# Hybrid SSD and attention layer on one core: small copies and constants change engines, and three pieces of side work change places

## The chip, the core and the metric

The kernel runs on one core of a Trainium2 chip. Its time is device time in microseconds (us), the median of several executions. A profile of one execution gives the times below; they count from the first instruction (the span). TensorE is PE in the profile, VectorE DVE, ScalarE ACT, GpSimd POOL, SyncE (which issues the DMAs) SP.

## What is computed

One decoder layer in float32 on 16 learned meta tokens and 1024 tokens of width 1024. Cut to what matters here:

```python
xn = rms_norm(h, mix_pre_g)                       # (1040, 1024)
z, xbc, dt_raw, q, k, v = split(xn @ w_in)
xbc = silu(causal_dwconv(xbc, conv_w, conv_b))    # 4 taps; x, B (2 groups), C (2 groups)
dt = softplus(dt_raw + dt_bias);  Acs = cumsum(dt * A)      # "decays", by chunk
y_ssd = rms_norm((intra_chunk(C, B, exp(seg(Acs)), x*dt) + C @ state * exp(Acs) + x*D) * silu(z))
beta = sigmoid(q @ k.T / 8)                       # stick breaking, strictly causal, 16 heads
w[t, s] = beta[t, s] * prod(1 - beta[t, j] for s < j < t)
y_sb = rms_norm(w @ v)
h = h + rms_norm(concat(y_ssd, y_sb) @ w_out)
h = h + rms_norm((gelu(causal_dwconv3(xn2 @ w_g)) * (xn2 @ w_u)) @ w_down)
```

## The kernel before

Every large product is made of three matmuls on a high and a low part of both operands. ACT makes the high part of a weight tile (whi, L182), POOL the low part (wlo, L183). Pairs of tiles are multiplied by a scheme of seven products in place of eight (class Duo); each product takes 24 matmuls of 128x260 and ends in an add on VectorE (L321) or a copy on ACT (L318). The raw result of a block that is convolved is a tile craw_* of 1043 columns, whose first three columns are zero.

The instructions of each engine run in the order in which the program writes them. A DMA of SP also stands in its queue, behind the DMAs written before it. The stages, in us of the span:

- 0 to 62: tokens are normed and transposed; the first blocks B0 and C0 are projected. Their convolutions remain to be done.
- 62 to 360: thirteen duos: x00, z00, x02, z02, bc, x10, z10, x12, z12 and four of q and k. While duo i runs its seven products, the list `slots` holds side work, `slots[j]` being issued behind product j. A convolution in it is cut into taps (L495 the first, L498 the others), a silu with a store (L502, L504) and three transposes with copies (`turns`). dt_acts is the softplus and the decays: `dts[3]` ends in L667, `dts[4]` to `dts[6]` are the decays (pz, L674) and a transpose of the cumulative sum (tacs).
- 360 to 449: the V projection.
- 449 to 605: the scan, 18 units of a group and a chunk. Its start makes three pairs of constants sl and sg, into which DMAs write the cumulative sums. A unit's weights are a difference of cumulative sums by matmul (sg, L1051), relu and exp on ACT (em), a matmul of C and B (cb, L1075) and a product on VectorE (em, L1081); yt (L1117) is their use. In between stand steps of a generator `fill` (the remaining q and k projections, pj_q and pj_k, six matmuls a step, 128 steps in all; SCAN_FILL sets how many a unit takes). A finished accumulator goes into a tile st: ACT makes the high part (L922), VectorE the low part (L928) or, with `via_sbuf`, ACT a copy sw (L925) and POOL the low part. A store (qkd<-st, L913) frees st. The tiles st are a ring of two, zk and xd (loads from L1037) rings of three.
- 605 to 905: the attention, 64 blocks (a pair of heads, 128 queries). A block's scores z (L1275) go through a sigmoid on ACT (kp, L1276) and a running product on VectorE (kp, L1279). Three blocks later comes its turn: transposes on TensorE (tw, L1296) and a copy of 1 - tw into th, on ACT for the first half (L1301), on VectorE for the second (L1299). th is the weight of the product with v (av, L1314). Further fill steps and pieces of the output projection stand between.
- 905 to 1734: output projection, FFN and down projection, in which the change does nothing.

Of the kernel before, what the change touches and what calls it, by code (L numbers as in the profile page):

```python
# [9 lines left out]
F32 = mybir.dt.float32  # L10
F32R = mybir.dt.float32r
BF16 = mybir.dt.bfloat16
AF = mybir.ActivationFunctionType
# [4 lines left out]
P = 128  # L18
# [17 lines left out]
QH = [QC[0], QC[2], QC[3], QC[1]]  # L36
NA = (NT + 1) * 16
NQA = 4
SCAN_FILL = 44
OUT_FILL = 14  # L40
FILL_AT = (2, 1)
BLOCKS = (7, 0, 6, 1, 5, 2, 4, 3)
# [25 lines left out]
def tile_layer(ctx: ExitStack, tc: tile.TileContext, x, meta, rows, parts,  # L68
# [158 lines left out]
    def raw_tile(nm, zero=False):  # L227
        raw = sr.tile([P, L + 3], F32, tag="cr", name=f"craw_{nm}", bufs=4)
        if zero:
            nc.gpsimd.memset(raw[:, 0:3], 0.0)  # L230
        return raw

    def conv_chain(nm, w, halves_=4):
# [498 lines left out]
    def merged(*lists):  # L732
        return [sum(parts_, []) for parts_ in zip(*lists)]

    c0_taps, _ = conv_acts(10, chains[1][0], "C0", None, bcd[0][1])
    dts = dt_acts()
    slots = [b0_taps[:2] + dts[0], b0_taps[2:4], b0_taps[4:] + c0_taps[:2], c0_taps[2:4], c0_taps[4:] + b0_turns[:1],
             b0_turns[1:2], b0_turns[2:], dts[1]]
    for i, q in enumerate(duos):
        n = duos[i + 1] if i + 1 < len(duos) else None  # L740
        if i + 2 < len(duos):
            duos[i + 2].load()
        for j, m in enumerate((1, 5, 2, 6, 7, 3, 4) if i == 0 else (1, 6, 5, 7, 2, 3, 4)):
            q.product(m)
            if i == 0:
                if m == 1:
                    d0.split_4()
                elif m == 6:
                    split_t(t4l.bitcast(F32), xo["t4"], nc.vector)
            if n is not None:  # L750
                if m == 1:
                    n.split_22()
                elif m == 6:
                    n.sums()
                elif m == 7:
                    n.split_3()
                elif m == 2:
                    n.split_1()
                elif m == 3:
                    n.split_4()  # L760
            elif m in (7, 2):
                v_split(1, int(m == 2))
            for act in slots[j]:
                act()
        extra = slots[7:]
        slots = q.done(q)
        for k, acts_ in enumerate(extra):
            slots[k] = acts_ + slots[k]
        if i == 1:
            slots = merged(slots, [[], dts[2], [], dts[3], [], [], dts[4]]) + [dts[5], dts[6]]  # L770
        if i == n_early:
            t_stack.close()
            vl = v_stack.enter_context(tc.tile_pool(name="vl", bufs=1, side="left"))
            fetch_v(1, 0, vl)
        if i + 2 == len(duos):
            fetch_v(0, 0, None)
# [138 lines left out]
    def qk_fill():  # L915
        def chain(n, qs):
            which, p = qk_blocks[n]

            def ev(acc, c0, m):
                put_stores()  # L920
                st = st_pool.tile([P, 2, CQ], F32R, tag="st", name=f"st{which}{p}{c0}")
                nc.scalar.activation(st[:, 0, :m], acc[:, :m], AF.Copy)  # L922
                if via_sbuf[0]:
                    raw = st_pool.tile([P, CQ], F32, tag="sw", name=f"sw{which}{p}{c0}", bufs=1)
                    nc.scalar.activation(raw[:, :m], acc[:, :m], AF.Copy)  # L925
# [58 lines left out]
    with tc.tile_pool(name="ssd", bufs=1, side="right") as sp:  # L984
# [22 lines left out]
        for b in range(3):  # L1007
            sl = sp.tile([32, P], F32R, tag=f"sl{b}", name=f"sl{b}")
            sg = sp.tile([32, 8, P], F32R, tag=f"sg{b}", name=f"sg{b}")
            nc.scalar.activation(sl, ones[:32], AF.Copy)  # L1010
            pick = sp.tile([32, 8], F32, tag="pick", name=f"pick{b}")
            nc.vector.tensor_tensor(pick, ident[:32, 16:24], ident[:32, 24:32], op=ALU.add)
            nc.scalar.activation(sg, pick.unsqueeze(2).to_broadcast([32, 8, P]), AF.Copy, scale=-1.0)
            segs.append((sl, sg))

        def load_bc(g, c):
# [14 lines left out]
        def load_zx(g, c):  # L1031
            a, b = (M0, NM) if c == 0 else (NM + (c - 1) * P, NM + c * P)
            y0 = M0 if c == 0 else 0
            zx = []
            for t, d in (("zk", zd), ("xd", xdd)):
                zx.append(sp.tile([P, 4, P], F32, tag=t, name=f"{t}{g}_{c}", bufs=3))
                nc.sync.dma_start(out=zx[-1][:, :, y0:y0 + b - a], in_=d[g][:, :, a:b].rearrange("b p t -> p b t"))  # L1037
            zxs[g, c] = zx

# [111 lines left out]
            run(fill, n * SCAN_FILL // 27 - (n - 1) * SCAN_FILL // 27)  # L1151

        load_bc(*units[0])
        nc.sync.dma_start(out=dtk, in_=dtkd)
        load_x(*units[0])
        load_state(0, 2)
        load_bc(*units[1])
        load_x(*units[1])
        load_bc(*units[2])
# [7 lines left out]
        for n, (g, c) in enumerate(units):  # L1167
# [13 lines left out]
            yt, zk, xd, prev[g] = chunk_outputs(g, c, *cur)  # L1181
            if nxt:
                chunk_mask(*units[n + 1], *nxt)
            via_sbuf[0] = int(n > 16)
            scan_fill()
            if late_sq:
                late_sq.pop(0)()
# [6 lines left out]
            elif n > 14:  # L1194
                load_q(n - 15)
            cur = nxt
        late_sq.pop(0)()
        chunk_sum(NT)

    roll = ExitStack()  # L1200
# [87 lines left out]
    def block_turn(p, i, bt, ths):  # L1288
        nm = f"{p}_{i}"
        for u in range(i // 4 + 1):  # L1290
# [4 lines left out]
                    c0 = (4 * u + b) * P  # L1295
                    nc.tensor.transpose(tw[:, j, b, :], bt[:, j, c0:c0 + P], ident)  # L1296
            th = ap.tile([P, 2, 4, P], F32, tag="th", name=f"th{nm}_{u}", bufs=4)
            if u:
                nc.vector.tensor_scalar(th[:, :, :nb, :], tw[:, :, :nb, :], -1.0, 1.0, op0=ALU.mult, op1=ALU.add)  # L1299
            else:  # L1300
                copied[0] = nc.scalar.activation(th[:, :, :nb, :], tw[:, :, :nb, :], AF.Copy,  # L1301
# [158 lines left out]
    def out_steps(half, t, w, y, evac):  # L1460
        yh, yl = y
        for hf in range(2):
            acc = psum_mm(f"mo{half}_{t}_{hf}")
            cs = slice(512 * hf, 512 * hf + 512)
            for k, (wh, wl) in enumerate(w):
                if k and k % 2 == 0:
                    yield 0
                for j, (u, v) in enumerate(((yh, wh), (yl, wh), (yh, wl))):
# [1 line left out]
            evac(acc, cs)  # L1470
            yield 1

    stage_tile = [lambda name: st_pool.tile([P, 2, CQ], F32R, tag="st", name=name).bitcast(F32)
                  .rearrange("p a b -> p (a b)")[:, :512]]

    def ssd_half(w, ys):
# [50 lines left out]
            closed[0] = next(work, 1)  # L1527

    shares = [FILL_AT[i % 2] * (4 if i < 2 else 1) for i in range(8 * NT)]
    total = 2 * (64 - 8 - SCAN_FILL) + 9 + 2 * OUT_FILL  # L1530

    def share(n):
        return round(total * sum(shares[:n]) / sum(shares))
# [5 lines left out]
    for step in range(8 * NT):  # L1539
# [12 lines left out]
        due = mix[:1]  # L1552
        if len(turn) >= TURN_LAG:
            run(begin_turn())
        if step == 0:
            some(5)
        block = block_weights(p, i)
        next(block, None)
        if p > 0 and n == 4:
# [891 lines left out]
```

## Time and profile before

| | |
|---|---|
| three executions, us | 1736.82, 1739.46, 1734.83 (median 1736.82) |
| the profiled execution, us | 1736.27 (span 1734.6, 1.7 around it) |
| busy: PE, DVE, ACT, POOL, us | 1672.1, 1098.9, 741.5, 768.1 |
| TensorE's mean granted clock | 0.991 |

A row of the waits gives who waited and on which line, for whom, the us in total, how often, and the longest. A row of the timeline gives the start, the us of that row, the engine, the line and tiles, and in brackets the idle time just before with what ended it; a row may join several instructions (x2). A group (by line and shape) gives the count, the busy us and mean ns, and behind the bar the idle time before. A row of windows gives a stretch, its length, the busy us of PE (and of PEld, DVE, ACT and POOL, where all engines are asked for), the clock granted to TensorE, where 1.00 is full, and the DMA's share and rate. Line numbers are those of the kernel before; in the changed kernel they are higher by 1 from about L1010 and by 2 from about L1240.

### The profile page before, as it was taken

To read this page: it belongs to the slowest core of one execution; us is meant where nothing else is said; L and a number is where in the kernel's file an instruction comes from. 1 tells how busy PE (TensorE), PEld (TensorE's weight loads), DVE (VectorE), ACT (ScalarE), POOL (GpSimd) and SP (SyncE) were. 2 spreads that over 40 slices of the span, in tenths; PEclk is the share of its full clock that TensorE was granted. 3 is DMA by queue.
4 is the path that set the end of the run, shared out by engine and by line. 5 is a ranking of instruction groups with operands and counts; after the bars stand their busy time and mean duration, and the time that the engine had idled before them with its cause. 6 is when DMAs were issued, how large, how long until landed. Compare 5 with 4: busy or idle time off the path is not lost.

```text
span 1734.6 us, 29010 instructions
## 1 busy us (share of the span) xinstructions
PE 1672.1 (96%) x11508; PEld 1438.2 (83%) x11508; DVE 1098.9 (63%) x1279; ACT 741.5 (43%) x1110; POOL 768.1 (44%) x591
## 2 busy tenths in 40 slices
PE   6899999999999999899999999999999999999998
PEld 5899999978777777677777788999998888888887
DVE  7756544354166687977771367676666656658777
ACT  6444344332244355655553344533333333344544
POOL 3665766620267452324322212487776677400001
PEclk9999999999899999999999999999999999999999
DMA  5334334434478764443422654233332222296335
GB/s 197 132 135 126 112 122 147 154 120 158 135 227 244 213 201 145 147 125 102 131 75 95 236 181 153 67 116 104 95 113 97 92 92 91 95 330 206 104 104 188
DMA packets 164522, 247.40 MB, mean 143 GB/s; under 512 B 18489, under 2 KB 99489, under 8 KB 162706
## 3 DMA queue, kind: packets, MB, share of 16 engines
q1 hardware_dynamic: 164386, 245.54, 43.9%
q8 instruction: 91, 1.49, 0.4%
q14 instruction: 45, 0.37, 0.1%
HBM read 162.00 MB, written 83.47 MB: 142 GB/s over the span
## 4 chain that ended last, share of the span: by engine, by line
PE 75%; DVE 5%; issue 4%; ACT 3%; POOL 2%; DMA 2%; SPq 0%; DVEq 0%; POOLq 0%; ACTq 0%
PE fX L1855 10%; PE mo L1469 10%; PE dnA L2267 7%; PE fY L1855 7%; PE fA L1855 7%; PE dnB L2267 5%; PE av L1314 3%; PE z L1275 2%; DVE kp L1279 2%; PE pj_k L219 2%; PE tw L1296 2%; PE dXqk L309 2%; PE vB L812 2%; PE pj_q L219 2%; PE dYqk L309 1%
## 5 line engine op out<-in xcount | busy, mean ns | idle before, releaser
L1279 DVE TENSOR_TENSOR_SCAN kp<-kp,hold 128x344 f32<-128x344 f32 (+6 forms) x224 | 198.1, 944 | 42.5 <-ACT kp L1276 42.1
L183 POOL TENSOR_TENSOR wlo<-wr,whi 128x1024 fp32r<-128x1024 f32 x43 | 99.3, 2319 | 41.0 <-ACT whi L182 37.5
L2304 POOL TENSOR_TENSOR fms<-fms 128x1 f32<-128x1 f32 x8 | 2.3, 288 | 222.0 <-DMA ar<-fda 185.9
L182 ACT ACTIVATE whi<-wr 128x1024 fp32r<-128x1024 f32 x43 | 45.7, 1062 | 112.2 <-PE fX L1855 73.5
L1927 DVE SCALAR_TENSOR_TENSOR ga<-gr,pp,ga 128x1024 f32<-128x1024 f32 x44 | 69.3, 1575 | 34.3 <-ACT ga L1920 33.6
L1254 POOL TENSOR_SCALAR cb<-kp 128x32 f32<-128x32 f32 x64 | 37.8, 591 | 117.1 <-DVE kp L1279 110.1
L2189 ACT ACTIVATE dh<-ar 128x512 fp32r<-128x512 f32 x77 | 48.6, 631 | 94.8 <-PE dnB L2267 44.7
L1276 ACT ACTIVATE kp<-z 128x688 f32<-128x688 f32 (+6 forms) x112 | 78.8, 736 | 14.9 <-PE z L1275 13.9
L1296 PE MATMUL tw<-ident,kp 128*128 128x128 f32 x576 | 76.8, 278 | 7.0 <-DVE th L1299 2.9
L2190 DVE TENSOR_TENSOR dl<-ar,dh 128x512 fp32r<-128x512 f32 x77 | 53.2, 691 | 47.2 <-ACT dh L2189 47.2
L1314 PEld LDWEIGHTS av<-th,v 128*64 128x64 f32 x1152 | 62.3, 138 | 22.4 <-issue 11.5
L1275 PE MATMUL z<-k,q 64*128 64x348 f32 (+8 forms) x672 | 75.2, 345 | 4.0 <-DVE th L1299 2.5
L1314 PE MATMUL av<-th,v 128*64 128x128 f32 x1152 | 77.8, 280 | 0.5 <-ACT ysc L1317 0.5
L1296 PEld LDWEIGHTS tw<-ident,kp 128*128 128x128 f32 x576 | 62.1, 141 | 17.1 <-issue 6.9
L1301 ACT ACTIVATE th<-tw 128x1024 f32<-128x1024 f32 x64 | 55.3, 864 | 34.5 <-PE tw L1296 33.1
L1275 PEld LDWEIGHTS z<-k,q 64*128 64x128 f32 x672 | 52.1, 186 | 20.9 <-issue 9.5
L2267 PE MATMUL dnA<-dl,dh 128*128 128x512 f32 x176 | 68.5, 389 | 0.0
L2267 PE MATMUL dnA<-dh 128*128 128x512 f32 x176 | 68.5, 389 | 0.0
L2267 PE MATMUL dnA<-dh,dl 128*128 128x512 f32 x176 | 68.5, 389 | 0.0
L1988 POOL TENSOR_TENSOR al<-wr,ah 128x512 fp32r<-128x512 f32 x20 | 28.6, 1432 | 77.5 <-ACT ah L1987 77.4
L2267 PE MATMUL dnB<-dh 128*128 128x512 f32 x132 | 51.3, 389 | 0.0
L2267 PE MATMUL dnB<-dh,dl 128*128 128x512 f32 x132 | 51.3, 389 | 0.0
(999 smaller groups left out, 6076.3 us busy)
## 6 DMA issues: line engine op xcount, KB each, us to landing
wr<-in_w_up SPq DMA_DIRECT2D x44, 512.0 KB
fds<-ga SPq DMA_DIRECT2D x44, 256.0 KB
b<-in_w_down SPq DMA_DIRECT2D x44, 256.0 KB
ar<-fds SPq DMA_DIRECT2D x44, 256.0 KB
fda<-ga SPq DMA_DIRECT2D x33, 256.0 KB
ar<-fda SPq DMA_DIRECT2D x33, 256.0 KB
k<-qkd SPq DMA_DIRECT2D x8, 1040.0 KB
q<-qkd SPq DMA_DIRECT2D x64, 128.0 KB
```

The source lines that it names most:

```text
L183: nc.gpsimd.tensor_tensor(l, raw, h.bitcast(F32), op=ALU.subtract)
L219: mm(acc[:, :CQ - s], a[:, k, :], b[:, k % 4, c + s:c + CQ], start=(k == 0 and j == 0), stop=(k == KB - 1 and j == 2))
L1275: mm(z[:, j, :w], u[h, :], r[h, a:a + w], start=s_ == 0, stop=s_ == 2)
L1276: nc.scalar.activation(kp[:, :, a:a + w], z[:, :, :w], AF.Sigmoid, scale=-QSCALE)
L1279: nc.vector.tensor_tensor_scan(part, part, hold[:, L - n + a:L - n + a + w][:, ::-1], 1.0 if ci == 0 else kp[:, j, a + w:a + w + 1], op0=A ...
L1296: nc.tensor.transpose(tw[:, j, b, :], bt[:, j, c0:c0 + P], ident)
L1301: copied[0] = nc.scalar.activation(th[:, :, :nb, :], tw[:, :, :nb, :], AF.Copy, scale=-1.0, bias=1.0).ins
L1314: mm(av[halves[j], :], v[:, kb, halves[j]], th[:, j, b, :], start=kb == 0, stop=kb == i)
L1469: recent[0] = mm(acc, u[:, k, :], v[:, cs], start=(k == 0 and j == 0), stop=(k == 7 and j == 2))
L1855: mm(acc[:, c, :nn], u[:, k, :], v[:, k, c0:c0 + nn], start=first and k == 0 and j == 0, stop=k == 3 and j == 2, skip_group_check=not first)
L1927: nc.vector.scalar_tensor_tensor(v, self.g[jj][:, :, i:i + 256], fconv_w[:, j, i:i + 1], v, op0=ALU.mult, op1=ALU.add)
L2267: mm(banks[BANK[n], t], u[:, 0, c], v[:, 1, :], start=(n in (1, 2, 5) and p == 0 and i == 0), stop=(p == NPR - 1 and i == 2), skip_group_c ...
```

## The change

1. The three zero columns of craw_* are written by ACT, no longer by POOL (12 instructions).
2. In the first duo the four taps of C0 stand two places later, and its silu with them.
3. The decays dts[4] to dts[6] stand one place later.
4. At the scan's start sl is written by POOL and sg by VectorE, both by ACT before; the loads of the states (B and C) stand ahead of the loads of dtk and x. st is a ring of three, xd a ring of two.
5. Of the fill steps, 82 stand inside the scan where 88 stood, and six at its end, ahead of chunk_sum; some(5) at the attention's first step is gone, and its steps come later in the same step, behind the first scores. Behind unit 16, VectorE makes the low parts where ACT's copy sw and POOL did.
6. The turn's second half is copied by VectorE only while left is 0. left is the number of finished halves of the last q and k block.

```diff
-SCAN_FILL = 44
+SCAN_FILL = 41
...
         if zero:
-            nc.gpsimd.memset(raw[:, 0:3], 0.0)
+            nc.scalar.activation(raw[:, 0:3], ones[:, 0:3], AF.Copy, scale=0.0)
...
-    slots = [b0_taps[:2] + dts[0], b0_taps[2:4], b0_taps[4:] + c0_taps[:2], c0_taps[2:4], c0_taps[4:] + b0_turns[:1],
-             b0_turns[1:2], b0_turns[2:], dts[1]]
+    slots = [b0_taps[:2] + dts[0], b0_taps[2:4], b0_taps[4:], [], c0_taps[:2] + b0_turns[:1],
+             c0_taps[2:4] + b0_turns[1:2], c0_taps[4:] + b0_turns[2:], dts[1]]
...
-            slots = merged(slots, [[], dts[2], [], dts[3], [], [], dts[4]]) + [dts[5], dts[6]]
+            slots = merged(slots, [[], dts[2], [], dts[3], [], [], []]) + [dts[4], dts[5], dts[6]]
...
-                st = st_pool.tile([P, 2, CQ], F32R, tag="st", name=f"st{which}{p}{c0}")
+                st = st_pool.tile([P, 2, CQ], F32R, tag="st", name=f"st{which}{p}{c0}", bufs=3)
...
-            nc.scalar.activation(sl, ones[:32], AF.Copy)
+            nc.gpsimd.tensor_copy(sl, ones[:32])
...
-            nc.scalar.activation(sg, pick.unsqueeze(2).to_broadcast([32, 8, P]), AF.Copy, scale=-1.0)
+            nc.vector.tensor_scalar(sg, pick.unsqueeze(2).to_broadcast([32, 8, P]), -1.0, None, op0=ALU.mult)
...
-                zx.append(sp.tile([P, 4, P], F32, tag=t, name=f"{t}{g}_{c}", bufs=3))
+                zx.append(sp.tile([P, 4, P], F32, tag=t, name=f"{t}{g}_{c}", bufs=3 if t == "zk" else 2))
...
         load_bc(*units[0])
+        load_state(0, 2)
         nc.sync.dma_start(out=dtk, in_=dtkd)
         load_x(*units[0])
-        load_state(0, 2)
...
-            via_sbuf[0] = int(n > 16)
             scan_fill()
...
+        run(fill, 1)
         late_sq.pop(0)()
+        run(fill, 5)
         chunk_sum(NT)
...
-            if u:
+            if u and not left[0]:
                 nc.vector.tensor_scalar(th[:, :, :nb, :], tw[:, :, :nb, :], -1.0, 1.0, op0=ALU.mult, op1=ALU.add)
...
-    total = 2 * (64 - 8 - SCAN_FILL) + 9 + 2 * OUT_FILL
+    total = 2 * (64 - 11 - SCAN_FILL) + 9 + 2 * OUT_FILL
...
-        if step == 0:
-            some(5)
```

On VectorE, in the first duo, from the first tap of C0 on (craw_x is the duo's raw tile, dXx and dYx two of its accumulators, t4l the low part of one of its operands, cdC the convolved C0):

```order
-L495 TENSOR_SCALAR cdC_929<-craw_C_452,pp 128x1040
-L498 SCALAR_TENSOR_TENSOR cdC_929<-craw_C_452,pp,cdC_929 128x1040
-L321 TENSOR_TENSOR craw_x_843<-dXx_932,craw_x_841 128x520
+L321 TENSOR_TENSOR craw_x_843<-dXx_929,craw_x_841 128x520
 L256 TENSOR_TENSOR t4l<-t4l,t4h 128x2080
-L498 SCALAR_TENSOR_TENSOR cdC_929<-craw_C_452,pp,cdC_929 128x1040 x2
-L321 TENSOR_TENSOR craw_x_841<-dXx_932,craw_x_841 128x520
+L321 TENSOR_TENSOR craw_x_841<-dXx_929,craw_x_841 128x520
+L495 TENSOR_SCALAR cdC_991<-craw_C_452,pp 128x1040
+L498 SCALAR_TENSOR_TENSOR cdC_991<-craw_C_452,pp,cdC_991 128x1040
 L321 TENSOR_TENSOR craw_x_843<-dYx_870,craw_x_843 128x520
```

The four taps of C0 stood ahead of two dXx adds; now the first two stand ahead of the dYx add, and the other two behind it.

In SP's queue at the scan's start (sl and sg are the constants, acsd and diagd the cumulative sums, bt and ct are B and C, xk is x):

```order
-L1020 DMA sl_4470<-acsd 8x128
-L1021 DMA sg_4471<-diagd_810 8x1024
-L1020 DMA sl_4470<-acsd 8x128
-L1021 DMA sg_4471<-diagd_811 8x1024
-L1154 DMA dtk_4463<-dtkd 128x720
-L1029 DMA xk_0_4493<-xsd_116 16x512
+L1021 DMA sl_4470<-acsd 8x128
+L1022 DMA sg_4471<-diagd_810 8x1024
+L1021 DMA sl_4470<-acsd 8x128
+L1022 DMA sg_4471<-diagd_811 8x1024
 L998 DMA bt_4464<-bcd_529 128x144
 L999 DMA ct_4465<-bcd_530 128x144
```

dtk and xk no longer stand ahead of bt and ct; they follow behind the eight loads of the states.

On ACT, around the first turn of the attention, before and then now (th are the turn copies, kp the sigmoids, ysc a copy of av, woab11h a part of the output weights):

```order
L922 ACTIVATE st_6430<-pj_k_0_260_6321 128x260
L925 ACTIVATE sw_6432<-pj_k_0_260_6321 128x260
L1301 ACTIVATE th_7_0_6452<-tw_7_0_6443 128x1024
L1276 ACTIVATE kp_1_6465<-z_1_0_6466 128x2x272
L1301 ACTIVATE th_0_0_6506<-tw_0_0_6503 128x2x128
L1276 ACTIVATE kp_5_6508<-z_5_0_6509 128x2x392
```

```order
L922 ACTIVATE st_6422<-pj_k_0_260_6345 128x260
L925 ACTIVATE sw_6424<-pj_k_0_260_6345 128x260
L1303 ACTIVATE th_7_0_6444<-tw_7_0_6435 128x1024
L1303 ACTIVATE th_7_1_6455<-tw_7_1_6446 128x1024
L1278 ACTIVATE kp_1_6457<-z_1_0_6458 128x2x272
L1303 ACTIVATE th_0_0_6498<-tw_0_0_6495 128x2x128
```

The second half's copy, th_7_1, stands right behind the first half's and ahead of the next block's sigmoid; on VectorE no turn copy is left (32 before), on ACT there are 96 (64 before).

More of the change, by code (lines that the diff above doesn't have):

```diff
@@ L1009, in tile_layer @@
             sg = sp.tile([32, 8, P], F32R, tag=f"sg{b}", name=f"sg{b}")
-            nc.scalar.activation(sl, ones[:32], AF.Copy)
-            pick = sp.tile([32, 8], F32, tag="pick", name=f"pick{b}")
-            nc.vector.tensor_tensor(pick, ident[:32, 16:24], ident[:32, 24:32], op=ALU.add)
-            nc.scalar.activation(sg, pick.unsqueeze(2).to_broadcast([32, 8, P]), AF.Copy, scale=-1.0)
+            nc.gpsimd.tensor_copy(sl, ones[:32])
+            if b == 0:
+                pick = sp.tile([32, 8], F32, tag="pick", name="pick")
+                nc.vector.tensor_tensor(pick, ident[:32, 16:24], ident[:32, 24:32], op=ALU.add)
+            nc.vector.tensor_scalar(sg, pick.unsqueeze(2).to_broadcast([32, 8, P]), -1.0, None, op0=ALU.mult)
             segs.append((sl, sg))
@@ L1471, in out_steps @@
             yield 1
-    stage_tile = [lambda name: st_pool.tile([P, 2, CQ], F32R, tag="st", name=name).bitcast(F32)
+    stage_tile = [lambda name: st_pool.tile([P, 2, CQ], F32R, tag="st", name=name, bufs=3).bitcast(F32)
                   .rearrange("p a b -> p (a b)")[:, :512]]
```

## The prediction, made before the changed kernel was run

> **What bounds the kernel now.** I read the engine totals first, then TensorE's waits, then its granted clock in short windows, and last the timeline around each long wait.
>
> ```profile
> PE 1672.1 (96%) x11508; PEld 1438.2 (83%) x11508; DVE 1098.9 (63%) x1279; ACT 741.5 (43%) x1110; POOL 768.1 (44%) x591
> core 0: 1734.6 us, clock 0.991
> ```
>
> TensorE is busy for 96%, and the change takes no matmul away. So it can gain only in the 62 us in which TensorE stands still and in the stretches at a lower clock. The waits of TensorE by line (us in total, times, longest) name the first kind:
>
> ```profile
> PE dXx L309 <- DVE craw_x L321: 3.9, 2, 3.1
> PE yt L1117 <- DVE em L1081: 3.2, 2, 2.0
> PE tw L1296 <- DVE th L1299: 2.9, 3, 1.4
> PE tw L1296 <- ACT th L1301: 2.7, 4, 1.5
> PE z L1275 <- DVE th L1299: 2.5, 4, 1.2
> PE dXx L309 <- POOL craw_x L230: 2.3, 2, 1.3
> PE pz L674 <- DVE s L667: 1.7, 1, 1.7
> PE pj_k L219 <- ACT sw L925: 1.6, 2, 0.8
> PE sg L1051 <- ACT st L922: 1.6, 1, 1.6
> ...
> PE tw L1296 <- ACT sw L925: 1.0, 1, 1.0
> PE yt L1122 <- DVE yt L1097: 1.0, 1, 1.0
> PE z L1275 <- ACT th L1301: 0.8, 3, 0.3
> ```
>
> The second kind is seen in windows of about 3.41 us (length, PE busy, granted clock, DMA share, GB/s):
>
> ```profile
> 83.91:87.32 3.41, 1.21 (x11) 1.00 0.00 0
> 87.32:94.15 6.83, 5.89 (x27) 0.50 0.50 142
> 452.55:459.37 6.82, 6.25 (x30) 0.50 0.37 73
> 462.79:466.20 3.41, 2.27 (x26) 1.00 0.54 157
> 466.20:469.60 3.40, 3.40 (x18) 0.50 0.50 84
> 596.00:599.40 3.40, 1.66 (x10) 1.00 0.53 149
> 623.22:626.63 3.41, 2.06 (x19) 1.00 0.99 325
> 626.63:630.04 3.41, 3.41 (x24) 0.50 0.48 133
> 708.55:711.96 3.41, 3.41 (x20) 0.50 0.74 224
> ```
>
> Behind a window in which TensorE stood for 1.1 to 2.2 us (3.41 - 2.27, 3.41 - 1.21) come one or two windows at half clock. It is no strict rule: 596.00 has 1.74 us of standing, and the clock stays. What a stretch at 0.50 costs is half of its busy time. A wait that goes can therefore pay twice, and I carry both payments apart.
>
> **Part A, C's taps in the first projection.** The 3.1 us wait lies in the first of these windows and a little beyond it. Around it stand (start, us, engine):
>
> ```profile
> 82.96 4.54 DVE L498 SCALAR_TENSOR_TENSOR cdC<-craw_C,pp,cdC 128x1040 f32<-128x1040 f32 x2
> ...
> 90.74 2.19 POOL L183 TENSOR_TENSOR wlo4z<-s24z,whi4z 128x1024 fp32r<-128x1024 f32 x1
> ...
> 99.29 0.39 PE L309 MATMUL dXz<-t2h,whi4z 128*128 128x260 f32 x1
> ```
>
> The add that frees dXx's buffer stands behind these two taps of C. In the new order it stands ahead of all four, right behind the t4l subtraction, which ends at 83.0, so TensorE would find its buffer free: -3.1. The taps then fall under products that do not wait for them. The dYx add stands behind two of them (4.54 at most), but no later product of this projection asks for its buffer. C's store goes later in SP's queue, and a small store of B's turn goes ahead of a weight load that only a later projection needs; both cost nothing as long as a projection of seven products covers them. What is late next is wlo4z: it is ready at 92.93, and dXz, 99.29 now, would come 3.1 and 2.9 (the clock, next) earlier, at 93.3. That cover is thin; I allow 0.2, and 2 us at the worst, should POOL be held up by the moved taps. The clock: 5.89 / 2 = 2.9 us are at stake from 87.32 to 94.15, and the wait is the whole of the idle time ahead; I take 2.5. **A = -2.9 - 2.5 = -5.4.**
>
> **Part B, decays a slot later.** pz waits 1.7 us for the last link of VectorE's softplus chain (L667). One product of 24 matmuls then stands between; 27 take 5.89 us at half clock above, so 24 at full clock some 2.6, and the wait goes: **-1.6** (0 if the chain is later itself). The transposes, copies and stores behind pz move with it, and nothing reads acst before the scan.
>
> **Memsets.** Twelve columns go from POOL to ACT.
>
> ```profile
> 120.44 2.18 POOL L183 TENSOR_TENSOR wlo4x<-s24x,whi4x 128x1024 fp32r<-128x1024 f32 x1 [4.43 <-ACT whi4x L182]
> 122.56 0.32 POOL L230 MEMSET craw_x<- 128x3 f32 x2
> L482 ACT ACTIVATE xtkX<-tt_X 16x128 f32<-16x128 f32 x8 | 2.0, 247 | 0.0
> ```
>
> The 2.3 us that the waits put down to this memset are not its own: at 122.56 it only follows wlo4x, which ends at 122.62 by its row, and it takes 0.1 (two in 0.32). So at most 0.2 is gained. On ACT a small operation takes 0.25; two of them stand in the head, where TensorE waits for copies: **+0.3** (0 to 3.0, 12 x 0.25).
>
> **Part C, the scan's start.**
>
> ```profile
> 447.17 1.04 ACT L1013 ACTIVATE sg<-pick 32x1024 fp32r<-32x1024 f32 x1
> 450.54 0.43 SPq L999 DMA_DIRECT2D ct<-bcd  x1
> 453.12 0.24 PE L1075 MATMUL cb<-ct,bt 128*16 128x16 f32 x2 [1.21 <-DMA ct<-bcd]
> ```
>
> Three sl on POOL and three sg on VectorE replace ACT's, of which sg alone takes 3 x 1.04. There is no row of the sg form on VectorE; its bounds are 0.4 (the smallest L1299 of part E, 392 ns for 128x256) and 2.3 (a tap of 128x1040 above), and I take ACT's 1.0, near L1299's 1.2 for as many elements a row. Then the segment's own DMA, which waits for the first sg (448.2 now), starts only 0.3 earlier: POOL makes its sl meanwhile, so sg needs not follow it; ACT is free for the q copies that stood behind its constants, and SP issues ct two loads sooner: dtk and xk (0.43 each by ct's row) plus the 0.3. The two waits, 1.6 and 1.2, lie one behind the other; I take the 0.3 and the 1.2, 1.5 of the 2.8. dtk and xk themselves are issued behind the eight loads of the states, some 8 x 0.43 = 3.4 later; POOL's xdt waits for them, and a weight split and em stand behind it on POOL. I cost that at nothing, since the same eight fill steps as before run first, and at 2 at the worst. Further, the third st buffer lets ACT's evacuation go on without waiting for a store; that store holds up the first of the two yt waits for em (3.2 less the longest, 2.0), since em on VectorE stands behind L928, which needs ACT's copy: -1.1. Clock: 6.25 / 2 = 3.1 at 452.55 with a chance of 0.4, since over 1 us of idle stays; 3.40 / 2 = 1.7 at 466.20, 0.5. **C = -1.5 - 1.1 - 1.2 - 0.9 = -4.7.** The xd ring falls to two buffers; its loads then wait for VectorE's product two units back. That is a new wait in SP's queue ahead of every load behind it, but that product is done about a unit's length, (605 - 449) / 18 = 8.7 us, before the tile is read. I take nothing; the worst of this part is 1 us in each of the 18 units.
>
> **Part D, the scan's end.**
>
> ```profile
> 590.91 6.84 DMA qkd<-st
> 597.84 0.39 ACT L922 ACTIVATE st<-pj_k 128x260 fp32r<-128x260 f32 x1 [5.45 <-DMA qkd<-st]
> ```
>
> A store of 6.84 us holds st, ACT waits 5.45 us for it, VectorE's L928 waits for ACT, and em (L1081), which yt needs, is queued behind. With three st buffers the 2.0 goes. The 1.0 of yt L1122 goes with the six projection steps put there, and so does pj_k's 1.6, since two buffers alternate; against it z_7_0 has to wait for the last evacuation, about 0.8 as pj_k did. **D = -2.0 - 1.0 - 1.6 + 0.8 = -3.8**, of which I count -3.0, since VectorE's chain into the attention starts only as early as q and k have landed.
>
> **Part E, turn copies in the attention.**
>
> ```profile
> L1299 DVE TENSOR_SCALAR th<-tw x32: 392/818/1226, 624.2 to 923.3; 128x1024 f32<-128x1024 f32 x8, 128x768 f32<-128x768 f32 x8, 128x512 f32<-128x512 f32 x8, 128x256 f32<-128x256 f32 x8
> L1301 ACT ACTIVATE th<-tw 128x1024 f32<-128x1024 f32 x40 | 40.9, 1023 | 23.3 <-PE tw L1296 23.3
> L1301 ACT ACTIVATE th<-tw 128x768 f32<-128x768 f32 x8 | 6.5, 809 | 3.4 <-PE tw L1296 3.4
> L1301 ACT ACTIVATE th<-tw 128x512 f32<-128x512 f32 x8 | 4.8, 606 | 1.4 <-POOL sq L1345 0.8 <-PE z L1275 0.5
> L1301 ACT ACTIVATE th<-tw 128x256 f32<-128x256 f32 x8 | 3.1, 385 | 6.4 <-PE tw L1296 6.4
> 605.00:760.00 155.00, 143.21 (x1411) 110.38 (x1410) 132.18 (x158) 92.99 (x151) 67.39 (x76) 0.98 0.54 159
> ```
>
> In this window VectorE (third pair) is busy for 132 of 155 us, ACT for 93. All 32 second halves leave VectorE, since the count of finished projections (left) stands at 1 before the first turn: 8 x (1.02 + 0.81 + 0.61 + 0.39) = 22.6 us more on ACT over 300 us, and VectorE's 32 x 0.8 = 26 us less. TensorE's waits for L1299 are 2.9 + 2.5 = 5.4, and the 1.0 of tw behind sw goes with the moved steps. The 64 copies on ACT cost 2.7 + 0.8 = 3.5 now, 0.055 each; 32 more at that rate, +1.8. Queued behind a copy on ACT are sigmoids (kp), for which VectorE's scans wait. Clock: 1.7 at 626.63 with 0.6 and 1.7 at 708.55 with 0.2, -1.4. **E = -5.4 - 1.0 + 1.8 - 1.4 = -6.0.**
>
> By the Trainium skill, page "ScalarE: Activation LUTs", section "Rules for kernel authors", a multiply or an add belongs on VectorE and not on ScalarE. The rows here (1.02 for ACT, up to 1.23 for VectorE, both out of PSUM) do not bear that out for these tiles; by the page the third rival would be the likelier.
>
> **The sum.** -5.4 - 1.6 + 0.3 - 4.7 - 3.0 - 6.0 = -20.4, of which the clock is 6.0 and waits are 14.4. A wait that goes lets TensorE run into the next one: of the pair 1.6 and 1.2 at the scan's start the second lies 0.6 us behind the first. I let a quarter of the 14.4 come back, +3.6. That is -16.8, against the profiled execution's 1736.3 us (its span of 1734.6 and 1.7 around it): 1719.5. The median shown, 1736.8, lies 0.5 above; I say **1720**.
>
> **The rivals.**
>
> First, the clock does not follow: as 596.00 shows, idle time doesn't decide alone, and shifted work may meet other windows; but all three drops whose window before is shown stand behind over 1.1 us of idle. Then only the waits and A's drop count: -14.4 + 3.6 - 2.5 = -13.3, 1723. Were A's drop to stay too, 1726 (1725.5). The page "TensorE: Matmul & The Clock Gate" of the Trainium skill, section "Why this matters for your kernels", lets the clock fall only behind gaps of over some 3 us, which here is A's alone; the trace does not agree, for a drop follows 1.14 us of idle at 462.79. By that rule C's and E's stretches would stay, 1723 again.
>
> Second, the gaps return: the weight splits on POOL, loads at the scan, or VectorE's scans of 0.9 us set the pace, and TensorE only waits elsewhere. For it speaks that the waits behind POOL's splits (the 2.3 above) are left as they are, and that in E VectorE stays at (132 - 13) / 155 = 77% in a chain of sigmoid, scan and turn; against it that A and D are single, long waits with nothing else late nearby. With a quarter of the waits and of the clock's 6.0 left, -3.6 - 1.5, it is 1731.
>
> Third, slower: ACT's queue. A second-half copy stands ahead of sigmoids in program order; if its time lands on the chain of sigmoid, scan and turn, TensorE pays up to 22.6 us in place of the 1.8. Everything else gives 16.8 + 1.8 = 18.6, so it decides where over 18.6 / 22.6 = 82% of every copy lies on the chain. With all of it and E's two clock stretches kept (1.4): 1736.3 + 4.0 + 1.4 = 1742; three new stretches at half clock (1.7 each) would make it 1747. For it: a sigmoid that waits a copy's 1.02 out is no rare thing with ACT at (93 + 13) / 155 = 68%. Against it: ACT stands idle for 62 of the 155 us now, and its 64 copies cost only the 0.055 each.
>
> Fourth, more: all five drops go and no wait comes back. At stake in the clock is 2.9 + 3.1 + 1.7 + 1.7 + 1.7 = 11.1, of which 6.0 is counted; -20.4 - 5.1 = -25.5: 1711.
>
> **How the numbers follow.** The sum as it stands 0.55, the clock not following 0.2, gaps returning 0.12, slower 0.05, more 0.08. A measurement tells about 0.3%, 5.2 us. Faster is 0.55 + 0.2 + 0.08 and a little of the second rival, 0.85; same 0.1; slower 0.05. The range runs from the fourth's 1711, less 1, to the second's near edge, 1732; what it leaves out is half of the second, the third and a little below, under 0.2.
>
> **What would show it.** Right: no wait over 1 us at dXx, pz, and at yt L1117; VectorE without th copies and ACT with 96; clock 1.00 from 87 to 94. Wrong: "z" and "tw" waiting for ACT's th for over 6 us; a wait for wlo4z over 1 us; cb still waiting 1.2 for ct; new windows at 0.50.

## The result, and the profile after

The changed kernel took 1724.0 us (median of five executions, 1723.4 to 1729.0) against 1736.8: a ratio of 0.9929, with a 95% interval from 0.9910 to 0.9948. A second series of six, taken later beside other kernels, gave 1726.3 and a ratio of 0.9936 (0.9921 to 0.9952). It is faster, by 10 to 13 us where 17 were forecast.

The profiled execution of the changed kernel is its slowest, 1729.0 us. Its engine totals and its clock:

```profile
PE 1673.6 (97%) x11508; PEld 1439.4 (83%) x11508; DVE 1083.7 (63%) x1250; ACT 753.3 (44%) x1146; POOL 770.8 (45%) x580
core 0: 1727.2 us, clock 0.989
```

TensorE's work is the same to 1.5 us. VectorE has lost 15 us of work and ACT has won 12. TensorE's waits, those that answer to the rows of before:

```profile
PE fX L1855 <- DVE gr L1906: 2.8, 1, 2.8
PE tw L1298 <- ACT th L1303: 2.7, 4, 1.5
PE dXx L309 <- POOL wlo4x L183: 2.5, 2, 1.3
PE yt L1118 <- DVE em L1082: 2.2, 1, 2.2
...
PE sg L1052 <- DMA bt<-bcd: 1.1, 1, 1.1
PE z L1277 <- DVE st L928: 1.0, 1, 1.0
...
PE pj_k L219 <- ACT sw L925: 0.8, 1, 0.8
PE z L1277 <- ACT th L1303: 0.8, 3, 0.3
PE dXx L309 <- DVE craw_x L321: 0.8, 1, 0.8
...
PE dXz L309 <- POOL wlo4z L183: 0.5, 1, 0.5
```

Gone are the 3.1 us of dXx, the 1.7 of pz, both rows of VectorE's th (5.4), one of the two waits of yt for em (the other has grown from 1.1 to 2.2), and half of pj_k's. The wait that was put down to the memset is there as before, 2.5 us where it was 2.3, now under its right name, wlo4x. The waits for ACT's copies have not grown in this profile: 2.7 and 0.8, as before. New are the first row, 2.8 us in the FFN, in which the change does nothing; 1.0 of z for the last evacuation; and, further down the list, 1.3 of the scan's states (st, L1102) for POOL's xw and 1.1 more of tt_X (1.5 where 0.4 stood), the small transposes of the convolved x.

The granted clock, in windows of the changed kernel:

```profile
82.05:85.46 3.41, 3.41 (x31) 1.00 0.12 44
85.46:92.28 6.82, 6.82 (x59) 1.00 0.31 88
92.28:95.70 3.42, 3.42 (x31) 1.00 0.35 133
95.70:99.12 3.42, 3.42 (x18) 0.50 0.60 244
454.11:457.52 3.41, 2.25 (x11) 1.00 0.79 145
457.52:464.34 6.82, 5.54 (x35) 0.50 0.68 193
693.04:699.86 6.82, 6.46 (x40) 0.50 0.73 216
```

From 82 to 95.7 the clock is full and TensorE never idle: the two windows at half clock of the first duo are gone. But a new one stands at 95.70, behind a window in which TensorE was busy throughout, and the scan's start and the attention have two each, where the kernel before had three at the scan's start and two in the attention. Three more that the profile of before has not stand at 232.24, 891.01 and 1129.94. Ahead of the first of them, from 228.83 to 232.24, TensorE is busy for 1.50 of 3.41 us: tt_X waits 0.7 there and wlo4x 1.25.

One profile doesn't tell what the clock does on the average. Each execution has its span and mean granted clock; (1 - clock) x span is the time that the clock took, counted as if TensorE were busy throughout, and I call it lost clock. The mean over the executions whose clock is on record:

| kernel | executions | mean time | lost clock | the rest |
|---|---|---|---|---|
| before | 61 | 1736.6 | 21.3 | 1715.3 |
| changed | 11 | 1726.0 | 17.4 | 1708.6 |
| C0's taps back | 11 | 1730.0 | 18.9 | 1711.2 |
| turn copies back on VectorE | 7 | 1727.8 | 17.8 | 1710.0 |
| scan back | 12 | 1734.1 | 20.8 | 1713.3 |
| decays and zero columns back | 12 | 1731.1 | 18.7 | 1712.4 |
| rings back | 10 | 1733.3 | 22.0 | 1711.3 |
| steps back | 6 | 1728.7 | 16.1 | 1712.6 |
| tpd twice | 6 | 1728.2 | 19.6 | 1708.6 |
| stores ahead | 6 | 1726.1 | 16.4 | 1709.7 |
| tpd in threes | 6 | 1727.0 | 17.0 | 1710.1 |
| second halves twice on ACT | 12 | 1735.9 | 20.7 | 1715.2 |
| stores ahead, squares on VectorE | 4 | 1722.4 | 15.1 | 1707.3 |

The kernel before ran beside each series, and its means there were 1736.3, 1736.7 and 1737.2. Of the gain of 10.6 in the means, 3.9 is clock and 6.7 is waits. The profile shown of before had lost 16.4, 5 less than its kernel's mean, and that of the changed kernel 19; side by side they would say that the clock got worse. Within a kernel single executions differ by up to 12 us, and mostly by their lost clock (its standard deviation is 1.3 to 5.7 in a series), so a mean of six is known to 1 or 2 us, and a difference of two rows of the table has a standard error of 1.1 to 1.7.

### The profile page after: what moved, and what is told of

Same layout as the page of the kernel before. It is cut to its first block, busy times and chain, and to the rows that moved or that the text cites. A ratio compares the mean times of both kernels' runs of the same rounds, so it can differ in the third digit from the quotient of the medians.

```text
span 1727.2 us, 29049 instructions
## 1 busy us (share of the span) xinstructions
PE 1673.6 (97%) x11508; PEld 1439.4 (83%) x11508; DVE 1083.7 (63%) x1250; ACT 753.3 (44%) x1146; POOL 770.8 (45%) x580
## 4 chain that ended last, share of the span: by engine, by line
PE 77%; issue 7%; POOL 5%; DMA 4%; DVE 4%; ACT 3%; SPq 1%; POOLq 0%; DVEq 0%; ACTq 0%
PE mo L1471 10%; PE fX L1855 10%; PE dnA L2267 7%; PE fY L1855 6%; PE fA L1855 6%; PE dnB L2267 5%; PE av L1316 3%; PE z L1277 3%; PE tw L1298 3%; PE dXqk L309 2%; PE vB L812 2%; PE pj_k L219 2%; PE dXx L309 2%; PE dYqk L309 1%; PE vA L812 1%
## 5 line engine op out<-in xcount | busy, mean ns | idle before, releaser
L1303 ACT ACTIVATE th<-tw 128x1024 f32<-128x1024 f32 (+2 forms) x96 | 74.6, 813 | 29.0 <-PE tw L1298 28.5
L498 DVE SCALAR_TENSOR_TENSOR cdX<-craw_x,pp,cdX 128x1040 f32<-128x1040 f32 x24 | 51.6, 2149 | 0.6
```

## The experiments

The theory after the result: the gain is TensorE's waits, removed part by part; windows at half clock follow in part and otherwise only move. The rivals were that a wait pays twice, as forecast, and that a part's wait was covered anyway. Four runs undo one part each; together they undo the whole change.

**C0's taps back.**

```diff
-    slots = [..., b0_taps[4:], [], c0_taps[:2] + b0_turns[:1], c0_taps[2:4] + b0_turns[1:2], ...]
+    slots = [..., b0_taps[4:] + c0_taps[:2], c0_taps[2:4], c0_taps[4:] + b0_turns[:1], ...]
```

> The changed kernel with C0's taps back where they stood in the first duo. Theory (the gain is TensorE's waits alone, part by part; half-clock windows only move): the 3.1 us wait of dXx is back, 1724.0 + 3.1 = 1727. Rival 1 (a wait pays twice, as in the forecast): 3.1 and 2.9 of clock, 1730. Rival 2 (the wait was hidden or comes back elsewhere): 1724.

Measured: median 1730.6 (ratio to before 0.9966, 0.9951 to 0.9981), in the means 4.0 over the changed kernel, 2.6 of it waits and 1.5 clock. Its profile in windows and its waits:

```profile
83.30:86.70 3.40, 2.00 (x18) 1.00 0.00 0
86.70:93.50 6.80, 5.05 (x42) 1.00 0.42 119
93.50:96.90 3.40, 3.40 (x31) 1.00 0.92 349
96.90:100.30 3.40, 3.40 (x17) 0.50 0.10 40
```

```profile
PE dXx L309 <- DVE craw_x L321: 3.9, 2, 3.2
PE dXx L309 <- POOL wlo4x L183: 1.2, 1, 1.2
```

The 3.2 is back, and here it lies across two windows, 1.4 in the first and 1.75 in the second: the clock stays full behind it. In the kernel before 2.2 of it fell into one window, and the clock fell. So the same wait cost 3 or 6 us by where it met the grid of windows, and that grid lies differently in every profile here. And one of the two waits for wlo4x (2.5 in the changed kernel) is gone: TensorE arrives later at the next duo, and POOL is ready. That isn't a rule: in the kernel before, with the taps in this same place and a wait of 3.1, wlo4x waits 1.26 at that point all the same.

**Second halves back on VectorE.**

```diff
-            if u and not left[0]:
+            if u:
```

> The changed kernel with the second halves of the turns copied by VectorE again. Theory: the waits of tw and z for VectorE's copies are back, up to 5.4 us, and the waits for ACT's copies stay near 3.5: 1729. Rival 1 (pays twice): two more windows at half clock, 1732. Rival 2 (a copy costs the same on either engine): 1724.

Measured: median 1728.3 (0.9956, 0.9940 to 0.9972), in the means 1.8 over the changed kernel. Its waits for copies:

```profile
PE tw L1298 <- ACT th L1303: 2.7, 4, 1.5
PE z L1277 <- ACT th L1303: 2.2, 4, 1.4
PE tw L1298 <- DVE th L1301: 1.6, 2, 1.3
PE z L1277 <- DVE th L1301: 0.9, 3, 0.4
```

2.5 us of VectorE's waits return, not 5.4. Perhaps the moved fill steps cover the others, since with them in place a late copy meets TensorE at other work; no run here shows that by itself. The sign is the theory's, the size is under half, and 1.8 is not clear of a standard error of 1.3.

**The scan back.**

```diff
-SCAN_FILL = 41
+SCAN_FILL = 44
...
-            nc.vector.tensor_scalar(sg, ..., -1.0, None, op0=ALU.mult)
+            nc.scalar.activation(sg, ..., AF.Copy, scale=-1.0)
...
-        load_state(0, 2)
         nc.sync.dma_start(out=dtk, in_=dtkd)
         load_x(*units[0])
+        load_state(0, 2)
...  # and the rings, sl, run(fill, 1), run(fill, 5), some(5), via_sbuf as before
```

> The changed kernel with the scan as before: constants on ACT, dtk and x loaded ahead of the states, st a ring of two and xd of three, 44 for SCAN_FILL, no steps at the scan's end, some(5) at the attention's start. Theory: between the V projection's end and the attention's first pta the changed kernel gained 5.1 us over the one before (9.0 less 3.9 in the two traces), so 1729. Rival 1 (the forecast's C and D, 7.7): 1732. Rival 2 (the steps are only moved, the scan is bound by loads): 1724.

Measured: median 1733.1 (0.9988, 0.9974 to 1.0003), in the means 8.1 over the changed kernel: 4.7 waits and 3.4 clock. Its profile has the old waits of the scan back, and in the attention 1.6 us of tw for sw:

```profile
PE yt L1117 <- DVE em L1081: 4.5, 2, 2.7
...
PE pj_k L219 <- ACT sw L925: 1.6, 2, 0.8
PE sg L1051 <- ACT st L922: 1.6, 1, 1.6
```

This part is the largest, and it comes to the forecast's C and D (7.7); the theory's 5.1, read from one pair of traces, left the clock out.

**Decays and zero columns back.**

```diff
-            slots = merged(slots, [[], dts[2], [], dts[3], [], [], []]) + [dts[4], dts[5], dts[6]]
+            slots = merged(slots, [[], dts[2], [], dts[3], [], [], dts[4]]) + [dts[5], dts[6]]
...
-            nc.scalar.activation(raw[:, 0:3], ones[:, 0:3], AF.Copy, scale=0.0)
+            nc.gpsimd.memset(raw[:, 0:3], 0.0)
```

> The changed kernel with the decays back in their place and the zero columns back on POOL. Theory: the wait of pz, 1.7 us, is back, and ACT's small operations, 0.3, go: 1725.4. Rival 1 (the memset on POOL held up TensorE, as the waits' row says): 2.3 more, 1727.7. Rival 2: nothing, 1724.

Measured: median 1730.8 (0.9973, 0.9958 to 0.9987), in the means 5.1 over the changed kernel; every expectation was too low. Its waits:

```profile
PE dXx L309 <- POOL craw_x L230: 2.4, 2, 1.3
PE pz L674 <- DVE s L667: 1.7, 1, 1.7
PE dXz L309 <- POOL wlo4z L183: 1.5, 1, 1.5
```

pz's 1.7 is back, and beside it dXz waits 1.5 for wlo4z, where the changed kernel waits 0.5: the weight split of a later duo is late again. The memset's row is 2.4, and with the copy on ACT it was 2.5: that rival has fallen. Which of the two edits makes wlo4z late was not tried apart. These two rows come to 2.7 us (1.7 and 1.0); where the rest of the 5.1 comes from was not found. Against it, tt_X's 0.7 at 229 is gone here, and the window at half clock behind it.

The four parts undone cost 4.0 + 1.8 + 8.1 + 5.1 = 19.0 us; undone together they cost 10.6. Each of these numbers is good to 1 or 2 us, so part of the difference is chance; that a wait that is back shelters a later one would explain the rest, but it is seen in one pair of profiles only (wlo4x above), and the kernel before doesn't agree.

**The changed kernel once more**, with no edit.

> The changed kernel itself once more, on the chip of the runs beside it, since single executions of all kernels spread by some 10 us and its first five lay within 6. Theory: 1724 to 1728, below each of the four kernels with a part undone (1728.3 to 1733.1). Rival: its first five runs were lucky, and it lies with them at 1728 to 1731; then the parts undone tell little apart.

Measured: median 1726.3, mean 1727.0. It lies below the four, as the theory says, though by less than its first five executions said. Its profile has the 2.8 us of fX again; of the thirteen profiles of changed kernels six have it, that of before has not. In the changed kernel's profile the chain of work shows where it starts:

```profile
1118.57 3.78 DMA fda<-ga
```

VectorE waits there for a store to land, and L1906, which TensorE needs, is queued behind. The same instructions are in all kernels; why the store is sometimes late was not found.

A second late transfer makes the first profile look better than it should. z waits 1.8 us for ACT's copies here, where it was 0.8, and in the ten other profiles with single copies 1.3 to 5.0. In all of them but tpd twice most of it is one wait, near 700 to 717 us, and ACT shows its cause (woabxl is a part of the output weights, wor the tile that is loaded for it):

```profile
707.10 1.15 ACT L1401 ACTIVATE woabxl<-wor,pp 128x1024 fp32r<-128x1024 f32 x1 [1.72 <-DMA wor<-in_w_out]
```

The turn copy is queued behind this instruction, which waits for a load: 1.1 to 3.5 us in these profiles, 0.3 in the first one of the changed kernel and in that of before. So a row "waits for ACT's th" is not always the price of a copy.

**The rings alone back.**

```diff
-                st = st_pool.tile([P, 2, CQ], F32R, tag="st", name=..., bufs=3)
+                st = st_pool.tile([P, 2, CQ], F32R, tag="st", name=...)
...  # and xd a ring of three
```

> The changed kernel with the rings as before (st of two, xd of three) and nothing else undone. Theory (a store of 7 us holds st at the scan's end): yt's wait of 2.0 for em is back at the scan's end, and the changed kernel's 1726 becomes 1728. Rival (the six steps taken out of the last units already keep st free): 1726, and no wait over 1 us of yt there.

Measured: median 1732.4 (0.9980, 0.9965 to 0.9996), in the means 7.3 over the changed kernel, of which 2.7 are waits and 4.6 clock. Its waits:

```profile
PE pj_k L219 <- DVE st L928: 2.8, 1, 2.8
...
PE z L1277 <- DVE st L928: 2.0, 1, 2.0
```

The 2.0 at the scan's end is back, but as a wait of z for the evacuation (L928) and not of yt for em, since the last steps now stand at the end; the expectation named the wrong waiter. The 2.8 is the same mechanism at the scan's start. By these means the rings carry most of the scan's gain, more than half of it as clock. st and xd were not tried apart.

**The steps alone back.**

```diff
-SCAN_FILL = 41
+SCAN_FILL = 44
...
-        run(fill, 1)
         late_sq.pop(0)()
-        run(fill, 5)
...  # and some(5) at the first step, via_sbuf behind unit 16
```

> The changed kernel with the projection steps as before (SCAN_FILL 44, none at the scan's end, some(5) at the attention's start, the copy sw behind unit 16), the rings of three and two kept. Theory: the waits at 617 and 624 of the kernel before (tw for sw, tw for th, 2.4 in all), of which the copy on ACT now takes the 1.35, are back in part, with pj_k's second 0.8: 1728. Rival (the steps' place matters for all of E's gain): 1731. Second rival: nothing, 1726.

Measured: median 1728.4 (0.9950, 0.9935 to 0.9965), in the means 2.7 over the changed kernel (waits 4.0, clock -1.3, with a standard error of 1.7 for the whole). The second 0.8 of pj_k comes back as part of 3.1, and the wait of tw for sw as it was:

```profile
PE pj_k L219 <- ACT sw L925: 3.1, 2, 2.3
...
PE tw L1297 <- ACT sw L925: 1.0, 1, 1.0
```

**tpd twice.** tpd's nine small products stand in the duo z00, ahead of the window that is at half clock at 95.70:

```profile
92.61 2.09 PE L641 MATMUL tpd<-fold,sq 32*16 32x16 f32 x18
```

```diff
-                mm(tpd[...], dtT[:, c0:c0 + nr], box["fold"], start=True, stop=True)
+                for _ in range(2):
+                    mm(tpd[...], dtT[:, c0:c0 + nr], box["fold"], start=True, stop=True)
```

> The changed kernel with every matmul of tpd (9 of 16 columns, about 2 us, in the duo z00) made twice. Theory (a window of 3.41 us in which TensorE streams few columns is followed by half clock, whether it stands still or runs small matmuls): 2 us more work, and always one or two windows at half clock from 96 on, 1.7 to 3.4: some 3 us over the changed kernel. Rival (only standing still lowers the clock, and tpd's dip in four of five traces is chance): 2 us over it, no window at half clock there.

Measured: median 1728.0 (0.9950, 0.9933 to 0.9967); in the means 2.2 over the changed kernel, by their lost clock, though the added 2 us of work must be in it too: these means are too coarse for that. Its windows tell more:

```profile
90.40:93.80 3.40, 3.40 (x34) 1.00 0.50 154
93.80:100.60 6.80, 6.80 (x33) 0.50 0.40 158
```

TensorE is busy for all of 90.40 to 93.80, from 91.33 on with matmuls of 16 columns in place of 260, and two windows at half clock follow where one did. That part of the theory holds, and standing still alone does not explain it. The twelve profiles with tpd as it was agree. In nine of them its 2.09 us lie inside one window of the grid (92.61 to 94.70 in 92.28:95.70 above), and half clock follows in all nine. In the other three the grid cuts them, into 0.29 and 1.80 (before), 1.88 and 0.21 (scan back) and 1.66 and 0.43 (stores ahead), and the clock stays full.

**tpd in threes.**

```diff
-            for i in range(NT + 1):
+            for i in range(3 * part, 3 * part + 3):
...
-             c0_taps[2:4] + b0_turns[1:2], c0_taps[4:] + b0_turns[2:], dts[1]]
+             ..., dts[1][:1], dts[1][1:2], dts[1][2:]]
```

> The changed kernel with the nine small matmuls of tpd in three threes behind the first three products of z00, where all nine stood behind the first. Same work, no wait taken away. Theory of streamed columns: the window at half clock at 96 goes, 1.7 us. Rival (standing still alone): no change there.

Measured: median 1727.0 (0.9943, 0.9929 to 0.9958), no gain (in the means 1.0 more). The window is gone, as the theory says, and a wait with another window at half clock behind it takes its place: VectorE is late with an add that is queued behind its softplus chain.

```profile
94.40:97.80 3.40, 3.40 (x29) 1.00 0.55 224
```

```profile
131.16 0.39 PE L309 MATMUL dYx<-b22h,whi4x 128*128 128x260 f32 x1 [2.42 <-DVE craw_x L321]
```

That is not the later end of the group: with tpd as it was and the stores ahead (the next run), the same wait stands at the same time.

```profile
131.08 0.39 PE L309 MATMUL dYx<-b22h,whi4x 128*128 128x260 f32 x1 [2.14 <-DVE craw_x L321]
```

The scan back has it too, 2.5. These are the three profiles of the new tap order without a window at half clock behind tpd: TensorE saves 1.7 us there and stands before VectorE's add instead. (tpd twice has the wait as well, 2.7.)

**Stores ahead at the scan's start.** In the changed kernel yt's wait of 2.2 starts at a store (SP's queue, ACT, TensorE):

```profile
453.97 0.61 SPq L913 DMA_DIRECT2D qkd<-st  x1
```

```profile
457.65 0.39 ACT L922 ACTIVATE st<-pj_q 128x260 fp32r<-128x260 f32 x1 [6.49 <-DMA qkd<-st]
457.93 0.25 ACT L1053 ACTIVATE em<-sg 16x128 f32<-16x128 f32 x1
```

```profile
458.80 1.04 PE L1118 MATMUL yt<-em,xdt 16*64 16x16 f32 x16 [2.21 <-DVE em L1082]
```

The fourth accumulator needs the first one's buffer; that one's store is issued at 453.97 only, behind all the loads of the scan's start, and ACT waits 6.49 us, with em's relu and exp queued behind.

```diff
         load_bc(*units[1])
+        run(fill, 8)
+        put_stores()
         load_x(*units[1])
         load_bc(*units[2])
         load_zx(*units[0])
         prev = [None, None]
-        run(fill, 8)
```

> The changed kernel with the stores of the first two q accumulators issued ahead of the second unit's x, the third unit's constants and the first z and x tiles at the scan's start. Theory (yt at the scan's start waits 2.2 us since st's first store stands behind these loads in SP's queue): that wait goes, 2.2, and the two windows at half clock behind it, 2.8: up to 5 us under the changed kernel. Rival 1: the wait goes and the clock stays, 2.2. Rival 2 (the loads behind the stores are then late): no gain.

Measured: median 1727.0 (0.9938, 0.9920 to 0.9955), the same as the changed kernel. The mechanism is right and the gain is not there: yt's wait is gone, and waits of st (L1102) for xw on POOL, 3.0 us where there were 1.3, have come.

```profile
PE st L1102 <- POOL xw L1062: 3.0, 3, 1.8
```

**Second halves twice on ACT.**

```diff
+                if u:
+                    nc.scalar.activation(th[:, :, :nb, :], tw[:, :, :nb, :], AF.Copy, scale=-1.0, bias=1.0)
                 copied[0] = nc.scalar.activation(th[:, :, :nb, :], tw[:, :, :nb, :], AF.Copy,
```

> The changed kernel with each of the 32 second-half copies made twice on ACT, one behind the other: 22.6 us more of ACT in the attention. Theory (ACT has slack there): waits of tw and z for ACT's copies grow by under 4 us; 1726 becomes 1727 to 1730. Rival (the forecast's third: a copy's time lies on the chain of sigmoid, scan and turn): up to 22.6 more, 1740 to 1749.

Measured: median 1736.0 (0.9994, 0.9983 to 1.0005), in the means 9.9 over the changed kernel, 6.6 waits and 3.3 clock. The theory's slack is too large and the rival's price too high: 44% of the 22.6 us lands on the end. z's waits grow most, from 0.8 and 1.8 in the two profiles of the changed kernel to 5.8, and here none of them is the single long one above:

```profile
PE z L1277 <- ACT th L1305: 5.8, 9, 0.9
```

So 32 more copies on ACT used up nearly all of the 10.6 that this change gave.

**Stores ahead, squares on VectorE.** The edit above, and:

```diff
-            nc.scalar.activation(sqt, flat, AF.Square)
+            nc.vector.tensor_tensor(sqt, flat, flat, op=ALU.mult)
```

> The changed kernel with the two stores ahead at the scan's start (as in the run that moved them alone) and with the squares of the attention's output (sqb, six of 128x1024, 1.06 us each) made by VectorE, no longer by ACT. Theory: the 2.2 of yt goes, and the 1.5 of tw at 692, where ACT makes a square, a copy and a weight ahead of th, shrinks by up to 1.0: 1722 to 1725. Rival: VectorE, the busier engine in the attention, pays for the squares in its scans: 1727.

Measured: median 1721.4 (0.9913, 0.9901 to 0.9926), the fastest of all, 3.6 below the changed kernel in the means of 4 and 11 executions. The two intervals still touch, so that it beats the changed kernel is likely and not shown. The 1.5 of tw went, and a single wait of z came, in this profile; ACT's copy stands there behind a part of the output weights that waits 2.96 us for its load, as above:

```profile
700.01 1.03 PE L1278 MATMUL z<-k,q 64*128 64x264 f32 x6 [3.61 <-ACT th L1304]
```

## Why the prediction was right, and where its sum was off

The forecast was faster, 1720 with a range of 1710 to 1732; 1724.0 and 1726.3 were measured. Of the gain of 16.8 a quarter to two fifths was not there. Of the prediction's own signs, the clock is at 1.00 from 87 to 94 and no wait is left at pz, as it asked; but yt waits 2.2 us, wlo4x over 1 (as it did before, under the memset's name), sg 1.1 for bt in place of cb's 1.2 for ct, and new windows at 0.50 have come. Step by step:

- **The base.** The sum was made against one profile whose lost clock (16.4) lay 5 below its kernel's mean. Both clock and waits are better compared by means over executions.
- **A (-5.4).** The add stands ahead of the taps and the wait is gone; wlo4z did not become late in that duo. Undone it costs 4.0. What the step left out is tpd's small matmuls, which bring half clock when they fall into one window: the window at 95.70 takes 1.7 back of the 2.9 that the first ones cost.
- **B (-1.6) and the memsets (+0.3).** pz's wait is gone, and the memset's row was not its own, as said. Undone together they cost 5.1, where 1.3 were forecast. A term left out is wlo4z's wait, 1.5 before and 0.5 after; the forecast had counted the waits behind POOL's splits as left as they are. With pz's 1.7 that is 2.7; the rest stays open, and the memsets' own price was not measured.
- **C (-4.7).** This is the step that failed. Its -1.1 for em and the clock behind it rested on a third st buffer that ends the wait at the scan's start; but four accumulators come before the first store has landed, and the wait grew from 1.1 to 2.2, with two windows at half clock behind it. The first two waits, 2.8, shrank to 1.1, 0.2 more than forecast. The clock's term there, 2.1, came out at 2.0 (3.1 and 1.7 before, 5.54 / 2 now), but by other windows, and that is luck. From the V projection's end to the fourth unit the changed kernel gains 2.0 in the traces. That the scan undone costs 8.1, near C and D together, does not bear the step out: 3.4 of it is clock.
- **D (-3.0).** Right: the waits there fell from 4.6 (2.0, 1.0, 1.6) to 2.2 (0.4 of yt for POOL, 0.8 of pj_k and the new 1.0 of z, which is the 0.8 that was set against it), so by 2.4. The third buffer does much of it: without it z waits 2.0 here.
- **E (-6.0).** The 5.4 is gone, and ACT's waits stayed at 3.5 in one profile and came to 4.5 in the other, where 5.3 was forecast. But undone it returns only 2.5 of waits and 1.8 of time. The copies' time is mis-sized a little: on ACT they take 74.6 us now and took 55.3, so 19.3 more and not 22.6. The price of 0.055 us a copy, from the 64 that were there, does not hold for yet more: 32 on top of these cost 9.9, or 0.31 each.
- **The clock (-6.0).** -3.9 in the means. The first rival, that the clock doesn't follow, is half right: in the profiles the two windows of A went and the scan's start has one less, but the attention has two as before and others came at new places.
- **What comes back (+3.6 of 14.4).** 6.7 of waits were gained, so 7.7 did not show: half and not a quarter. Of the 6.2 by which the gain fell short in the means, 4.1 is this term and 2.1 the clock. In the traces of the two kernels C's st accounts for 2.2 (+1.1 where -1.1 was forecast), POOL's xw for 1.3 and tt_X for 1.1; wlo4z's 1.0 goes the other way.
- **Slower by ACT's queue.** It did not happen; its point was put at 82% of a copy's time on the chain, and the doubled copies show 44%.

By the page "TensorE: Matmul & The Clock Gate" of the Trainium skill, section "Why this matters for your kernels", the clock falls behind gaps of over some 3 us. The traces here don't agree: a window with 2.25 of 3.41 us busy (454.11) has half clock behind it, and so has one that is busy throughout and ends in small matmuls (90.40), while the gap of 3.2 us with C0's taps back left the clock full.

## What to carry to other kernels

Price a removed wait by what TensorE meets next, not by its length: here half of the waits that were to go did not show in the time. A ring needs a buffer for every result that is made before the first store is issued, so the store's place in the queue counts beside the number of buffers: three were not enough for four results, and with the stores ahead they were. Read what the engine that is waited for was itself waiting for: z's row of ACT's copies held a late load. Where the granted clock costs 15 to 22 us an execution, compare means of many executions and their granted clocks; one pair of profiles can have the sign wrong.

## What the runs showed of the hardware

For the clock, TensorE's matmuls of 16 columns count as idle time, or nearly: 2.09 us of them inside one window of 3.41 us brought half clock behind it in nine profiles of nine, at most 1.88 us of them inside one window left the clock full in three of three, and twice as many brought two windows. What a wait costs in clock depends on how it falls on the grid of windows: 3.2 us across two of them cost nothing, 2.2 in one cost 2.9. Executions of one kernel lay up to 12 us apart, mostly by their lost clock.
